# Down-projections of a two-layer encoder trunk: block sums T2 and T4 formed in the up-projections, last operands loaded earlier and split later

## Chip, cores and metric

The kernel runs on one core of a Trainium2 chip. The metric is the device time of one execution in microseconds (us), the median of several runs. The engines are PE (matrix multiplications, with PEld for the loading of its weights), DVE (VectorE, element by element on two operands), ACT (ScalarE, here mostly rounding copies), POOL (GpSimd, here almost only the issuer of accumulating transfers) and SP (the issuer of all other transfers). Each takes its own instructions in order and waits for the others by semaphores.

## What is computed

A sequence of 1024 frames of width 1024 goes through two layers. Each ends in a gated MLP with a causal convolution:

```python
def conv_ffn(h, w_up, conv_w, conv_b, w_down):
    s = h.shape[1]
    u = h @ w_up
    up = jnp.pad(u, ((0, 0), (CONV_WIDTH - 1, 0), (0, 0)))
    conv = conv_b
    for j in range(CONV_WIDTH):
        conv = conv + conv_w[j] * up[:, j:j + s]
    a, g = jnp.split(conv, 2, axis=-1)
    return (jax.nn.silu(a) * g) @ w_down

def reference(...):
    for layer in range(DEPTH):
        ...
        x = x + conv_ffn(rms_norm(x, ffn_norm[layer]), ffn_w_up[layer], ffn_conv_w[layer],
                         ffn_conv_b[layer], ffn_w_down[layer])
    return x
```

The hidden width is 2816, that is 22 blocks of 128 rows. The rest (a stick-breaking attention with a pooling mixer in layer 0, a gated linear attention in layer 1) is not touched here.

## The kernel before

**Splitting.** Every factor of a product is held as a rounded high part and a low part (float32 less the rounded value). A product is three matmuls: high by high, high by low, low by high. A *split* is one CAST on ACT (the high part) and one subtraction on DVE (the low part), in this order.

**Seven products instead of eight.** Both the up- and the down-projection treat their factors as 2x2 blocks and compute seven block products (Winograd's form). For the down-projection the blocks of the right factor are the halves in time (T0, T1, 512 frames each) of an even and an odd block of the hidden layer. With B11 and B12 the halves of the even block and B21 and B22 those of the odd one, the sums are T1 = B12 - B11, T3 = B22 - B12, T2 = T3 + B11 and T4 = T3 + (B11 - B21). A product sums over 11 pairs of blocks, j = 0 to 10.

**Up-projection, `ffn`.** The loop over i makes hidden block i by seven products on PE (class `Pair`, lines 979 to 1005 evacuate them), the convolution (L1038 on ACT, L1039 and L1041 on DVE) and the gate. In an even i, L1175 makes `even` and L1176 T1; B11 and T1 are written to DRAM. In an odd i, L1182 makes the odd block in `ca`, L1183 U = B11 - B21 and L1184 T3, both in `cg`; L1186 writes B21 and B22 as one tile `b2` and L1187 writes U and T3 as one tile `ut3`. One i lasts about 19.4 us.

**Down-projection, `down`.** `order` runs through six products P1, P5, P6, P3, P7, P4, each with steps j = 0 to 10: 66 steps of 12 matmuls (L1266). `prep` of step number i + 3 is written ahead of step i: it fetches the operands (L1211, tags `rb` for the right block, `rw`, `rs` and `ra` for the left ones, four buffers each for `rb` and `rw`), forms the left operand on DVE (`left`: L1226 for P5, L1229 for P6, L1235 for P3, L1237 for P7) and splits both in `split_block` (L1195 ACT, L1196 DVE) into tiles `blk` of a pool of 16 buffers. The right operand comes from the table `right`. Where the table names two sources, the second is added in flight: POOL issues an accumulating transfer (L1213) that has to wait until the first one has landed. P6 takes T3 and adds B11; P4 takes T3 and adds U.

The seventh product needs, as its left operand, four *rows* of the odd weight blocks (`last_left`, L1293 to L1295; a tile `wraw` of 8 blocks and a tile `r3` of 3, in pieces of 512 bytes) and as its right operand the eleven B21 (`last_right`, L1278 to L1282, two at a time). Rows 0 and 1 are loaded and split at P6's steps 2 and 6; the B21 from P7's step 8 to P4's step 7. The final loop multiplies them (L153 to L157).

When a product's 11 steps are done, four additions (eight behind P7) put its PSUM banks into x (L1270).

**Order.** PE follows the program as written throughout, and SP does so inside `down`. ACT and DVE are ordered by a scheduler that works from its own estimate of the times when the program is built. So a change in one place can move instructions on DVE and ACT elsewhere.

Of the kernel before, what the change touches and what calls it, by code (L numbers as in the profile page):

```python
# [57 lines left out]
def trunk_kernel(  # L58
# [952 lines left out]
    def ffn(layer, nm, after, ow, mixt, onward=None):  # L1011
# [107 lines left out]
        for i in range(FT):  # L1119
            nx = i + 1 < FT  # L1120
            ca, cg = cs_[2 * i % 3], cs_[(2 * i + 1) % 3]
            if i == 0:
                ua, ug = us[0], us[1]
            elif i == 1:
                ua, ug = us[2], us[0]
                for cs, b in zip(HALVES, ps):
                    V.tensor_tensor(ug[:, cs], b, rstd_bc[:, cs], op=ALU.mult)
            else:
                further = i + 2 < FT
                if i == 2:  # L1130
# [24 lines left out]
                scaled(ug[:, T0], T0)  # L1155
                q, p = p, None
                if nx:
                    p = Pair(i + 1)
                    p.P1()
                q.P3()  # L1160
                if nx:
                    split_s34()
                if further:
                    load_s4(i + 2)
                scaled(ua[:, T1], T1)
            if i == 1:
                for ld in loads:
                    ld(i + 2)
            conv(FT + i, ug, cg)
            conv(i, ua, ca)  # L1170
            S.activation(ca, ca, AF.Silu)


            if i % 2 == 0:
                V.tensor_tensor(even, ca, cg, op=ALU.mult)  # L1175
                V.tensor_tensor(ca[:, T0], even[:, T1], even[:, T0], op=ALU.subtract)  # L1176
                b11, t1 = (dram.tile([P, 512], F32, tag=f"{n}{layer}_{i}", name=n) for n in ("b11", "t1"))
                nc.sync.dma_start(b11, even[:, T0])
                nc.sync.dma_start(t1, ca[:, T0])
                blocks.append({"B11": b11, "T1": t1})  # L1180
            else:
                V.tensor_tensor(ca, ca, cg, op=ALU.mult)  # L1182
                V.tensor_tensor(cg[:, T0], even[:, T0], ca[:, T0], op=ALU.subtract)  # L1183
                V.tensor_tensor(cg[:, T1], ca[:, T1], even[:, T1], op=ALU.subtract)  # L1184
                b2, ut3 = (dram.tile([P, T], F32, tag=f"{n}{layer}_{i}", name=n) for n in ("b2", "ut3"))
                nc.sync.dma_start(b2, ca)  # L1186
                nc.sync.dma_start(ut3, cg)  # L1187
                blocks[-1].update(B21=b2[:, T0], B22=b2[:, T1], U=ut3[:, T0], T3=ut3[:, T1])
        ev.close()

        down(layer, blocks, ready, after, onward)

    def split_block(src):
        t = hpool.tile([P, T], R32, tag="h", name="blk")
        S.copy(t[:, 0:512], src)  # L1195
        V.tensor_sub(t[:, 512:T], src, t[:, 0:512].bitcast(F32))  # L1196
        return t

    def down(layer, blocks, ready, after, onward):

# [5 lines left out]
        NJ = FT // 2  # L1206
        w = [(wdn[layer, 2 * j], wdn[layer, 2 * j + 1]) for j in range(NJ)]

        def fetched(tag, src, add=None, bufs=4):
            t = dn.tile([P, 544 if tag == "rb" else 512], F32, tag=tag, name=tag, bufs=bufs)[:, 0:src.free_size()]  # L1210
            nc.sync.dma_start(t, src)  # L1211
            if add is not None:
                G.dma_start(t, add, accum_op=ALU.add)  # L1213
            return t

        a11, s = [None] * NJ, [None] * NJ
# [20 lines left out]
                V.tensor_tensor(t, a11[j], t, op=ALU.subtract)  # L1237
            return t


        right = {"P1": ("B11",), "P5": ("T1",), "P6": ("T3", "B11"), "P3": ("B22",), "P7": ("T3",), "P4": ("T3", "U")}

        def prep(n, j):
            if n == "P1" and j < len(ready):
                return ready[j]
            rb = fetched("rb", *(blocks[j][b] for b in right[n]))
            if n == "P1":
                load_a11(j)
            return split_block(left(n, j)), split_block(rb)
# [23 lines left out]
        b21 = []  # L1273

        def last_right(js):
            raw = hpool.tile([P, T], R32, tag="h", name="b21").bitcast(F32)
            for cs, j in zip(HALVES, js):
                nc.sync.dma_start(raw[:, cs], blocks[j]["B21"])  # L1278
                hi = dn.tile([P, 512], R32, tag="ra", name="b21h", bufs=NJ)
                lo = dn.tile([P, 512], R32, tag="rs", name="b21l", bufs=NJ)  # L1280
                S.copy(hi, raw[:, cs])
                V.tensor_sub(lo, raw[:, cs], hi.bitcast(F32))  # L1282
                b21.append((hi, lo))

        odd = wdn[layer].rearrange("(f two) p k -> two p f k", two=2)[1]

        def last_left(r):
            parts = []
            big = (hpool, ("wraw", "h", "h"), (1, 16, 16)) if r == KT // 2 - 1 else (wpool, ("wraw", "whi", "wlo"), (1, 2, 2))
            for k0, k1, (pool, tags, nb) in ((0, KT, big), (KT, NJ, (dn, ("r3", "r3h", "r3l"), (1, 2, 2)))):  # L1290
                raw, hi, lo = ((wpool if t == "wraw" else pool).tile([P, (k1 - k0) * P], d, tag=t, name=t, bufs=b)
                               for t, d, b in zip(tags, (F32, R32, R32), nb))
                nc.sync.dma_start(raw.rearrange("p (f k) -> p f k", k=P), odd[:, k0:k1, r * P:(r + 1) * P])  # L1293
                S.copy(hi, raw)
                V.tensor_sub(lo, raw, hi.bitcast(F32))  # L1295
                parts += [(hi[:, sl], lo[:, sl]) for sl in (slice(k * P, (k + 1) * P) for k in range(k1 - k0))]
            return parts
# [47 lines left out]
        for r in range(half):  # L1345
# [389 lines left out]
```

## Time and profile before

| | us |
|---|---|
| median of 3 runs | 2199.06 (2197.35 to 2202.14) |
| the profiled execution | 2199.35 |
| its span in the profile | 2197.7 |
| up-projection and down-projection, layer 0 | up from about 494, six products of `down` from 881.4 |
| up-projection and down-projection, layer 1 | up from about 1570, six products of `down` from 1968.5 |
| granted TensorE clock, mean | 0.996 |

All times below are microseconds from the span's start. A row of the timeline has start, duration, engine, line, operation, output and inputs, form, count; in brackets stands the idle time of the engine ahead of it and what ended it. Durations overlap: an instruction starts before the one ahead of it has fully ended, so the distance between starts, not the duration, is what a queue of them costs. A row of the waits has who waited for whom, the total in us, how often, and the longest.

### The profile page before, as it was taken

How to read it: one execution, taken by the hardware profiler on the slowest of the kernel's cores; microseconds unless marked ns; L12 is line 12 of the kernel's file. 1: busy time of each engine (PE TensorE's matmuls, PEld its weight loads, DVE VectorE, ACT ScalarE, POOL GpSimd, SP SyncE). 2: the span in 40 equal slices, each digit the busy share in tenths (PEclk: the TensorE clock that was granted, in tenths of full speed). 3: DMA queues.
4: the chain of work that ended last, by engine and by line, in shares of the span. 5: the costliest groups of instructions: out<-in, count | busy, mean ns of one | idle time of the engine just before them, and what ended most of it. 6: DMA issues, size and time to landing. Idle time of an engine off the chain costs nothing.

```text
span 2197.7 us, 28082 instructions
## 1 busy us (share of the span) xinstructions
PE 2150.8 (98%) x10384; PEld 1767.0 (80%) x10384; DVE 1664.8 (76%) x2458; ACT 1093.1 (50%) x1705; POOL 162.1 (7%) x188
## 2 busy tenths in 40 slices
PE   8999989999999999999999999999999999999998
PEld 7889878888878888778887878787788888887776
DVE  5687688698989899777736655557898998987763
ACT  6666566464444444344546362637544444443441
POOL 2240120000000000010000000000000000000110
PEclk9999999999999999999999999999999999999999
DMA  4132332353444434987501111105343444449885
GB/s 152 49 107 87 94 112 94 119 130 106 130 119 126 124 116 124 350 216 233 169 21 40 38 49 38 49 30 145 105 124 116 123 122 120 124 157 327 222 239 157
DMA packets 126201, 280.31 MB, mean 128 GB/s; under 512 B 13408, under 2 KB 27360, under 8 KB 126064
## 3 DMA queue, kind: packets, MB, share of 16 engines
q1 hardware_dynamic: 112528, 251.25, 34.9%
q0 software_dynamic: 13536, 27.27, 7.0%
q8 instruction: 81, 1.33, 0.2%
q14 instruction: 56, 0.46, 0.1%
HBM read 208.21 MB, written 54.53 MB: 120 GB/s over the span
## 4 chain that ended last, share of the span: by engine, by line
PE 61%; DMA 15%; DVE 15%; issue 4%; ACT 4%; SPq 1%; POOL 0%; DVEq 0%; ACTq 0%; POOLq 0%
PE lin L936 10%; PE z L936 7%; PE lin L153 4%; PE lin L155 4%; PE lin L157 4%; DMA rb<-ut 4%; PE t L936 3%; PE d L936 3%; DMA rw<-in_wdn 3%; DVE blk L1196 2%; PE z L157 2%; PE z L153 2%; PE z L155 2%; DMA raw_g<-in_wup 2%; DMA wraw<-in_wup 2%
## 5 line engine op out<-in xcount | busy, mean ns | idle before, releaser
L1038 ACT ACTIVATE c<-u,prm 128x1024 f32<-128x1024 f32 x88 | 109.1, 1244 | 86.7 <-DVE u L964 79.1
L1266 PE MATMUL lin<-blk 128*128 128x512 f32 x396 | 118.6, 400 | 14.0 <-ACT blk L1195 8.6
L1196 DVE TENSOR_TENSOR blk<-rb,blk 128x512 fp32r<-128x512 f32 x124 | 85.1, 686 | 53.9 <-ACT blk L1195 53.4
L153 PE MATMUL lin<-h_hi,whi 128*128 128x512 f32 x288 | 114.2, 432 | 6.6 <-ACT whi L139 6.0
L1039 DVE SCALAR_TENSOR_TENSOR c<-u,prm,c 128x1023 f32<-128x1023 f32 x88 | 112.3, 1278 | 8.5 <-ACT c L1038 8.5
L1195 ACT CAST blk<-rb 128x512 fp32r<-128x512 f32 x124 | 76.6, 618 | 81.2 <-DMA rb<-ut 44.0
L936 PE MATMUL d<-T,a 128*128 128x512 f32 x480 | 115.4, 389 | 0.0
L1041 DVE SCALAR_TENSOR_TENSOR c<-u,prm,c 128x1022 f32<-128x1022 f32 x88 | 112.3, 1276 | 0.0
L1266 PE MATMUL t<-blk 128*128 128x512 f32 x396 | 112.0, 391 | 0.0
L1266 PE MATMUL d<-blk 128*128 128x512 f32 x396 | 111.9, 391 | 0.0
L1266 PE MATMUL z<-blk 128*128 128x512 f32 x396 | 111.6, 390 | 0.0
L964 DVE TENSOR_TENSOR u<-u,rstd_bc 128x512 f32<-128x512 f32 x160 | 107.8, 684 | 0.4
L936 PEld LDWEIGHTS d<-T,a 128*128 128x128 f32 x480 | 90.1, 188 | 18.7
L155 PE MATMUL lin<-h_lo,whi 128*128 128x512 f32 x288 | 104.4, 398 | 0.7 <-DVE h_lo L264 0.7
L1266 PEld LDWEIGHTS lin<-blk 128*128 128x128 f32 x396 | 73.0, 189 | 39.8 <-ACT blk L1195 13.2
L157 PE MATMUL lin<-h_hi,wlo 128*128 128x512 f32 x288 | 104.2, 398 | 0.0
L936 PE MATMUL z<-blk,s34h 128*128 128x512 f32 x320 | 101.3, 398 | 1.4 <-DVE u L995 1.4
L936 PE MATMUL z<-blk,s12h 128*128 128x512 f32 x320 | 100.9, 396 | 0.0
L936 PE MATMUL lin<-T,s34h 128*128 128x512 f32 x320 | 99.5, 392 | 0.8 <-ACT tm L986 0.8
L936 PE MATMUL t<-blk,whi 128*128 128x512 f32 x320 | 99.6, 392 | 0.0
L936 PE MATMUL lin<-blk,whi 128*128 128x512 f32 x320 | 99.5, 392 | 0.0
L936 PE MATMUL lin<-T,s12h 128*128 128x512 f32 x320 | 99.4, 391 | 0.0
(516 smaller groups left out, 6021.0 us busy)
## 6 DMA issues: line engine op xcount, KB each, us to landing
wraw<-in_wup SPq DMA_DIRECT2D x44, 512.0 KB, 3.7
rw<-in_wdn SPq DMA_DIRECT2D x88, 256.0 KB, 4.7
raw_g<-in_wup SPq DMA_DIRECT2D x40, 512.0 KB, 3.8
rb<-ut SPq DMA_DIRECT2D x66, 256.0 KB, 4.4
b<-c SPq DMA_DIRECT2D x22, 512.0 KB, 2.6
ut<-c SPq DMA_DIRECT2D x22, 512.0 KB, 3.8
s<-in_wup SPq DMA_DIRECT2D x40, 256.0 KB, 2.6
s<-s POOLq DMA_DIRECT2D x40, 256.0 KB, 4.4
```

The source lines that it names most:

```text
L153: PE.matmul(out[i], wh, ah[i], start=first, stop=False)
L155: PE.matmul(out[i], wh, al[i], start=False, stop=False)
L157: PE.matmul(out[i], wl, ah[i], start=False, stop=last)
L936: PE.matmul(ps, w, m, start=first and k == 0 and n == 0, stop=k == 3 and n == 2, skip_group_check=True)
L964: V.tensor_tensor(dst, dst, rstd_bc[:, cs], op=ALU.mult)
L1038: S.activation(c, u, AF.Identity, scale=pcol(b + 2), bias=pcol(b + 3))
L1039: V.scalar_tensor_tensor(c[:, 1:], u[:, :T - 1], pcol(b + 1), c[:, 1:], op0=ALU.mult, op1=ALU.add)
L1041: V.scalar_tensor_tensor(c[:, 2:], u[:, :T - 2], pcol(b), c[:, 2:], op0=ALU.mult, op1=ALU.add)
L1195: S.copy(t[:, 0:512], src)
L1196: V.tensor_sub(t[:, 512:T], src, t[:, 0:512].bitcast(F32))
L1266: PE.matmul(ps, l, m, start=first and j == 0 and i == 0, stop=j == NJ - 1 and i == 2, skip_group_check=True)
```

## The change

Three parts. First, the odd i of the up-projection forms T4 = U + T3 in place of U and T2 = B11 + T3 in place of `even`'s first half, by two more additions on DVE, and writes T4 and T3 as one tile `t43` and T2 as a tile `t2` of its own. The table `right` then has one source per product, and the accumulating transfers of `down` are gone. Second, `last_left` and `last_right` only issue their transfers and return a function `later` that does the splits. Row 0 is loaded at P5's step 6 and split at P6's step 6, row 1 loaded at P3's step 1 and split at P3's step 10 (rows 2 and 3, in the final loop, are split at once as before). The B21 are loaded from P7's step 2 on and split four steps later, from P7's step 6 to P4's step 5. Third, these splits are traced inside `behind_latest`, which puts them on ACT and DVE behind the split of the latest `prep`. That is an order of issue alone; nothing waits for the completion of the split ahead.

```diff
+                V.tensor_tensor(cg[:, T0], cg[:, T0], cg[:, T1], op=ALU.add)
+                V.tensor_tensor(even[:, T0], even[:, T0], cg[:, T1], op=ALU.add)
-                nc.sync.dma_start(ut3, cg)
-                blocks[-1].update(B21=b2[:, T0], B22=b2[:, T1], U=ut3[:, T0], T3=ut3[:, T1])
+                nc.sync.dma_start(t43, cg)
+                nc.sync.dma_start(t2, even[:, T0])
+                blocks[-1].update(B21=b2[:, T0], B22=b2[:, T1], T4=t43[:, T0], T3=t43[:, T1], T2=t2)
...
     def split_block(src):
-        S.copy(t[:, 0:512], src)
-        V.tensor_sub(t[:, 512:T], src, t[:, 0:512].bitcast(F32))
+        a = S.copy(t[:, 0:512], src)
+        b = V.tensor_sub(t[:, 512:T], src, t[:, 0:512].bitcast(F32))
+        latest[:] = a.ins, b.ins
...
+    def behind_latest():
+        st = ExitStack()
+        for ins in latest:
+            st.enter_context(tc.issue_after(ins))
+        return st
...
-            if add is not None:
-                G.dma_start(t, add, accum_op=ALU.add)
...
-        right = {"P1": ("B11",), "P5": ("T1",), "P6": ("T3", "B11"), "P3": ("B22",), "P7": ("T3",), "P4": ("T3", "U")}
+        right = {"P1": "B11", "P5": "T1", "P6": "T2", "P3": "B22", "P7": "T3", "P4": "T4"}
...
-            if n == "P6" and j in (2, 6):
-                rows[j // 4] = last_left(j // 4)
-            k = NJ * (n == "P4") + j - 8
-            if n in ("P7", "P4") and k % 2 == 0 and 0 <= k < NJ + 1:
-                last_right(range(k, min(k + 2, NJ)))
+            if (n, j) in LATER:
+                with behind_latest():
+                    due.pop(0)()
+            if (n, j) in ROWS:
+                due.append(last_left(ROWS.index((n, j))))
+            k = NJ * (n == "P4") + j - 2
+            if n in ("P7", "P4") and k % 2 == 0 and 0 <= k < NJ + 5:
+                if k > 3:
+                    with behind_latest():
+                        due.pop(0)()
+                if k < NJ + 1:
+                    due.append(last_right(range(k, min(k + 2, NJ))))
```

with `ROWS, LATER = [("P5", 6), ("P3", 1)], [("P6", 6), ("P3", 10)]`. Lines of the changed kernel are shifted: L1195, L1196 of `split_block` become L1199, L1200; L1211 becomes L1225; L1226 and L1229 become L1238 and L1241; L1270 becomes L1281; L1293 to L1295 become L1309 to L1318.

Three places where the order of instructions moves. SP, from the last steps of P5 in layer 0 into P6, before (`t` are the T1, `ut` the tiles with T3):

```order
L1211 DMA rb<-t_7423 128x512
L1211 DMA rs<-in_wdn 128x512
L1211 DMA rw<-in_wdn 128x512
L1211 DMA rb<-ut_4931 128x512
L1211 DMA rb<-ut_5209 128x512
L1211 DMA rb<-ut_5470 128x512
L1211 DMA rb<-ut_5731 128x512
L1211 DMA rb<-ut_5992 128x512
L1211 DMA rb<-ut_6253 128x512
L1293 DMA wraw<-in_wdn 128x8x128
L1293 DMA r_8168<-in_wdn 128x3x128
```

and now (`t_4934` and on are the T2):

```order
L1225 DMA rw<-in_wdn 128x512
L1309 DMA wraw<-in_wdn 128x8x128
L1309 DMA r_8047<-in_wdn 128x3x128
L1225 DMA rb<-t_7463 128x512
L1225 DMA rs<-in_wdn 128x512
L1225 DMA rw<-in_wdn 128x512
L1225 DMA rb<-t_4934 128x512
L1225 DMA rb<-t_5216 128x512
L1225 DMA rb<-t_5481 128x512
```

Row 0's two transfers now stand ahead of the three of P5's last step (j = 10) and of all of P6's.

ACT in P6 of layer 0 (`blk<-rs` and `blk<-rb` are a step's two splits), before:

```order
L1195 CAST blk<-rs 128x512
L1294 CAST whi<-wraw 128x1024
L1195 CAST blk<-rb 128x512
L1195 CAST blk<-rs 128x512
L1294 CAST r3h<-r_8168 128x384
L1195 CAST blk<-rb 128x512
L1195 CAST blk<-rs 128x512
```

and now:

```order
L1199 CAST blk<-rb 128x512
L1317 CAST whi<-wraw 128x1024
L1317 CAST r3h<-r_8047 128x384
L1199 CAST blk<-rs 128x512
L1199 CAST blk<-rb 128x512
L1199 CAST blk<-rw 128x512
```

Before, row 0 was split between the casts of P6's steps 4 and 5; now between those of its steps 9 and 10, the last ahead of P3's first (`blk<-rw`).

DVE at the start of P5 in layer 0 (`rs<-rs,rw` forms a step's left operand for P5, `rs<-rs,ra` the one for P6 later, `x<-x,...` are the four additions behind P1), before:

```order
L1229 TENSOR_TENSOR rs<-rs,ra 128x512
L1270 TENSOR_TENSOR x<-x,lin 128x512
L1226 TENSOR_TENSOR rs<-rs,rw 128x512
L1270 TENSOR_TENSOR x<-x,z 128x512
L1270 TENSOR_TENSOR x<-x,t 128x512
L1270 TENSOR_TENSOR x<-x,d 128x512
L1196 TENSOR_TENSOR blk<-rs,blk 128x512
L1196 TENSOR_TENSOR blk<-rb,blk 128x512
L1226 TENSOR_TENSOR rs<-rs,rw 128x512
L1229 TENSOR_TENSOR rs<-rs,ra 128x512
L1196 TENSOR_TENSOR blk<-rs,blk 128x512
L1226 TENSOR_TENSOR rs<-rs,rw 128x512
```

and now:

```order
L1238 TENSOR_TENSOR rs<-rs,rw 128x512
L1200 TENSOR_TENSOR blk<-rs,blk 128x512
L1200 TENSOR_TENSOR blk<-rb,blk 128x512
L1241 TENSOR_TENSOR rs<-rs,ra 128x512
L1281 TENSOR_TENSOR x<-x,lin 128x512
L1281 TENSOR_TENSOR x<-x,z 128x512
L1281 TENSOR_TENSOR x<-x,t 128x512
L1281 TENSOR_TENSOR x<-x,d 128x512
L1238 TENSOR_TENSOR rs<-rs,rw 128x512
L1200 TENSOR_TENSOR blk<-rs,blk 128x512
L1200 TENSOR_TENSOR blk<-rb,blk 128x512
L1238 TENSOR_TENSOR rs<-rs,rw 128x512
```

Step 1 is now split ahead of the additions, and step 2's left operand is formed only behind all four.

More of the change, by code (lines that the diff above doesn't have):

```diff
@@ L1184, in ffn @@
                 V.tensor_tensor(cg[:, T1], ca[:, T1], even[:, T1], op=ALU.subtract)
-                b2, ut3 = (dram.tile([P, T], F32, tag=f"{n}{layer}_{i}", name=n) for n in ("b2", "ut3"))
+                V.tensor_tensor(cg[:, T0], cg[:, T0], cg[:, T1], op=ALU.add)
+                V.tensor_tensor(even[:, T0], even[:, T0], cg[:, T1], op=ALU.add)
+                b2, t43, t2 = (dram.tile([P, n], F32, tag=f"{s}{layer}_{i}", name=s)
+                               for s, n in (("b2", T), ("t43", T), ("t2", 512)))
                 nc.sync.dma_start(b2, ca)
-                nc.sync.dma_start(ut3, cg)
-                blocks[-1].update(B21=b2[:, T0], B22=b2[:, T1], U=ut3[:, T0], T3=ut3[:, T1])
+                nc.sync.dma_start(t43, cg)
+                nc.sync.dma_start(t2, even[:, T0])
+                blocks[-1].update(B21=b2[:, T0], B22=b2[:, T1], T4=t43[:, T0], T3=t43[:, T1], T2=t2)
         ev.close()
@@ L1245, in prep @@
                 return ready[j]
-            rb = fetched("rb", *(blocks[j][b] for b in right[n]))
+            rb = fetched("rb", blocks[j][right[n]])
             if n == "P1":
@@ L1278, in last_right, with later @@
                 nc.sync.dma_start(raw[:, cs], blocks[j]["B21"])
[L1279 to L1283, printed above, removed]
+            def later():
+                for cs, j in zip(HALVES, js):
+                    hi = dn.tile([P, 512], R32, tag="ra", name="b21h", bufs=NJ)
+                    lo = dn.tile([P, 512], R32, tag="rs", name="b21l", bufs=NJ)
+                    S.copy(hi, raw[:, cs])
+                    V.tensor_sub(lo, raw[:, cs], hi.bitcast(F32))
+                    b21.append((hi, lo))
@@ L1285, in down @@
+            return later
         odd = wdn[layer].rearrange("(f two) p k -> two p f k", two=2)[1]
         def last_left(r):
-            parts = []
             big = (hpool, ("wraw", "h", "h"), (1, 16, 16)) if r == KT // 2 - 1 else (wpool, ("wraw", "whi", "wlo"), (1, 2, 2))
+            raws = []
             for k0, k1, (pool, tags, nb) in ((0, KT, big), (KT, NJ, (dn, ("r3", "r3h", "r3l"), (1, 2, 2)))):
-                raw, hi, lo = ((wpool if t == "wraw" else pool).tile([P, (k1 - k0) * P], d, tag=t, name=t, bufs=b)
-                               for t, d, b in zip(tags, (F32, R32, R32), nb))
+                raw = (wpool if tags[0] == "wraw" else pool).tile([P, (k1 - k0) * P], F32, tag=tags[0], name=tags[0], bufs=1)
@@ L1293, in last_left, with later @@
                 nc.sync.dma_start(raw.rearrange("p (f k) -> p f k", k=P), odd[:, k0:k1, r * P:(r + 1) * P])
[L1294 to L1297, printed above, removed]
+                raws.append((raw, pool, tags, nb))
+            def later():
+                parts = []
+                for raw, pool, tags, nb in raws:
+                    n = raw.free_size()
+                    hi, lo = (pool.tile([P, n], R32, tag=t, name=t, bufs=b) for t, b in zip(tags[1:], nb[1:]))
+                    S.copy(hi, raw)
+                    V.tensor_sub(lo, raw, hi.bitcast(F32))
+                    parts += [(hi[:, sl], lo[:, sl]) for sl in (slice(k * P, (k + 1) * P) for k in range(n // P))]
+                rows[r] = parts
@@ L1299, in down @@
+            return later
         LEAD = 3
@@ L1305, in down @@
         half = KT // 2
-        rows = {}
+        rows, due = {}, []
+        ROWS, LATER = [("P5", 6), ("P3", 1)], [("P6", 6), ("P3", 10)]
         for i, (n, j) in enumerate(order):
@@ L1350, in down @@
             if r + 2 < half:
-                rows[r + 2] = last_left(r + 2)
+                last_left(r + 2)()
             if r == 0:
```

3 lines of the change are left out of this document (2 added, 1 removed).

## The prediction

> **What bounds the kernel now.** I read the page first, then PE's timeline at the ends of the products, then who waits.
>
> ```profile
> span 2197.7 us, 28082 instructions
> PE 2150.8 (98%) x10384; PEld 1767.0 (80%) x10384; DVE 1664.8 (76%) x2458; ACT 1093.1 (50%) x1705; POOL 162.1 (7%) x188
> ```
>
> PE is busy for 98% of the span, so a change that leaves the matmuls alone can only win what PE loses in gaps. Its timeline gives these gaps by product: the first matmul of P5, P6, P3, P7, P4 and of the final loop (L153) in layer 0, then P5, P6, P3, P4 and the final loop in layer 1.
>
> ```profile
> 911.30 0.84 PE L1266 MATMUL lin<-blk 128*128 128x512 f32 x3
> 943.80 0.84 PE L1266 MATMUL lin<-blk 128*128 128x512 f32 x3
> 980.81 0.84 PE L1266 MATMUL lin<-blk 128*128 128x512 f32 x3
> 1010.73 0.84 PE L1266 MATMUL lin<-blk 128*128 128x512 f32 x3
> 1040.65 0.84 PE L1266 MATMUL lin<-blk 128*128 128x512 f32 x3
> 1071.27 0.40 PE L153 MATMUL lin<-b21h,whi 128*128 128x512 f32 x1
> ...
> 1998.47 0.84 PE L1266 MATMUL lin<-blk 128*128 128x512 f32 x3
> 2030.41 0.84 PE L1266 MATMUL lin<-blk 128*128 128x512 f32 x3
> 2066.53 0.84 PE L1266 MATMUL lin<-blk 128*128 128x512 f32 x3
> 2126.37 0.84 PE L1266 MATMUL lin<-blk 128*128 128x512 f32 x3
> 2162.43 0.40 PE L153 MATMUL lin<-b21h,whi 128*128 128x512 f32 x1
> ```
>
> P3 and P7 in layer 0 take 980.81 to 1010.73 and 1010.73 to 1040.65, both 29.92 for 11 steps, 2.72 a step: PE without a gap. What the others take above 29.92 is lost. Layer 0: P5 32.50, so **2.6**; P6 37.01, **7.1**; P4 30.62, **0.7**. Layer 1: P5 31.94, **2.0**; P6 36.12, **6.2**; P4 36.06, **6.1**. Together 24.7 us. That is all there is to win in these products, and the three parts of the change aim at P6 and P4.
>
> **Why P6 and P4 lose.** Two of the waits inside layer 1's six products:
>
> ```profile
> POOL rb L1213 <- DMA rb<-ut: 29.6, 10, 4.5
> ACT blk L1195 <- DMA rb<-ut: 25.0, 11, 7.4
> ```
>
> POOL waits 29.6 us for the first source of a right operand before it may issue the second (up to 4.5 each); ACT then waits 25.0 for the accumulating transfer (in P4 it too is named `rb<-ut`), up to 7.4. A right block is thus two landings, up to 11.9 of waiting, and has one of four `rb` buffers meanwhile: 11.9 / 4 is over PE's 2.72. That is P4's bound and the base of P6's. P6 has a second burden; ACT, PE and a window of layer 0:
>
> ```profile
> 966.54 1.05 ACT L1294 CAST whi<-wraw 128x1024 fp32r<-128x1024 f32 x1 [1.38 <-DMA wraw<-in_wdn]
> 969.72 0.62 ACT L1195 CAST blk<-rb 128x512 fp32r<-128x512 f32 x1 [2.13 <-DMA rb<-b]
> 970.39 0.50 PE L1266 MATMUL lin<-blk 128*128 128x512 f32 x1 [2.08 <-ACT blk L1195]
> 972.00:1002.00 30.00, 30.00 (x127) 24.66 (x126) 26.81 (x45) 15.90 (x29) 0.00 (x0) 0.94 0.74 234
> ```
>
> Row 1's split sits at the head of ACT's queue and waits 1.38 for its row, with a step's casts behind it; PE stands for 2.08 at 970.39. Behind that gap the granted clock is 0.94 over 30 us (last row, third number from the end): 0.06 x 30 = 1.8 of the 7.1 are slow matmuls.
>
> The Trainium skill's "TensorE: Matmul & The Clock Gate", Part 1, says that the clock is gated down after an idle window of about 3.4 us. This trace shows it behind a gap of 2.08. By the page those 1.8 would have another cause and could stay: the sum below would come out 1.8 higher.
>
> **Part by part.**
>
> *Accumulating transfers gone (22 per layer).*
>
> ```profile
> rb<-ut SPq DMA_DIRECT2D x66, 256.0 KB, 4.4
> ```
>
> A right block is one landing again, 4.4 by the page's median, as in P3 and P7, which have the same splits, one more DVE operation per step, and lose nothing. P6 then fetches one block of 256 KB a step where P3 fetches two. POOL has no other work in `down`. I take P4's loss (0.7 + 6.1) as gone, and P6's with the next item. Ends: none of it, or all, 20.1 with P6.
>
> *Rows 0 and 1 split behind later steps.* Same instructions, so no new work; their rows have long landed, so ACT no longer waits with casts behind it. P6's 7.1 + 6.2 = 13.3 goes. What is late next: at P6's start the splits have little lead, but without transfers to wait for a split pair is 1.2 on DVE against 2.72 on PE, so the lead grows each step. Behind the moved splits on ACT and DVE stand P6's step 10 and P3's step 0, some steps ahead of PE by then.
>
> *Row 0's load moved into P5.* It stands on SP ahead of the loads of P5's step 10 and all of P6's. A row's landing in layer 1's tail (last number), the DMA engines at P5's end in layer 0 (share 0.28), and step 10's left operand, from issue to landing and then on DVE:
>
> ```profile
> wraw<-in_wdn SPq DMA_DIRECT2D x1, 512.0 KB, 5.2
> 934.00:936.00 2.00, 1.77 (x8) 1.18 (x7) 2.00 (x4) 1.08 (x3) 0.00 (x0) 1.00 0.28 106
> 930.03 3.89 DMA rw<-in_wdn
> 936.79 0.68 DVE L1226 TENSOR_TENSOR rs<-rs,rw 128x512 f32<-128x512 f32 x1
> ```
>
> Step 10's `rw` landed at 933.92 and DVE took it at 936.79, 2.9 spare. If the row holds step 10 up for its full landing of 5.2, it costs 5.2 - 2.9 = 2.3 a layer; at the other end nothing. I take nothing: DVE itself is later there (next item), and part of the row fits into that idle stretch. Row 1 and the B21 move into P3 and P7, whose steps need 2.72 on PE with the DMA share at 0.74 (the 972 to 1002 row): nothing, up to 2.3 a layer if not.
>
> *DVE's order in P5.* P5's loss is not the transfers': DVE waits for one only twice, at its first steps. That wait, then DVE from step 6 to 7 and at step 8, then PE at step 8, all in layer 0:
>
> ```profile
> DVE rs L1226 <- DMA rw<-in_wdn: 3.1, 2, 2.7
> 926.41 0.69 DVE L1226 TENSOR_TENSOR rs<-rs,rw 128x512 f32<-128x512 f32 x1
> 927.86 0.69 DVE L1196 TENSOR_TENSOR blk<-rs,blk 128x512 fp32r<-128x512 f32 x1 [0.76 <-ACT blk L1195]
> 928.47 0.69 DVE L1196 TENSOR_TENSOR blk<-rb,blk 128x512 fp32r<-128x512 f32 x1
> 929.07 0.69 DVE L1229 TENSOR_TENSOR rs<-rs,ra 128x512 f32<-128x512 f32 x1
> 929.67 0.68 DVE L1226 TENSOR_TENSOR rs<-rs,rw 128x512 f32<-128x512 f32 x1
> ...
> 934.99 0.68 DVE L1196 TENSOR_TENSOR blk<-rb,blk 128x512 fp32r<-128x512 f32 x1
> 935.73 0.73 PE L1266 MATMUL lin<-blk 128*128 128x512 f32 x2 [0.23 <-DVE blk L1196]
> ```
>
> A sum followed at once by its own split waits 1.45 (926.41 to 927.86) for ACT's cast in between, and the step costs 929.67 - 926.41 = 3.26 against PE's 2.72: 0.54 lost. With another operation in between it costs 0.60 per operation. PE's second matmul starts 0.74 behind the start of the right block's subtraction (934.99 to 935.73). Before, steps 4 to 7 were of the slow kind. The new order has 1, 2, 4 to 7 and 10, and all four additions to x ahead of step 2's sum. Laid out from the same first landing with these distances, layer 0's right blocks of steps 2, 4 and 8 are subtracted at 917.1, 923.0 and 936.0, and the last of P5 lets P6 start at 944.7, 0.9 later than 943.80. The same for layer 1 gives 2030.8 against 2030.41, **+0.4**. So +1.3. Ends: all eleven steps slow, 11 x 0.54 = 5.9 a layer, +3.3 and +3.9; or P5 without loss, -4.6. I take the layout, as the order is fixed when the program is built.
>
> *The two additions.* 22 pairs x 2 x 0.60 = 22 x 1.2 = 26.4 us of DVE in the up-projections. DVE in one odd i, and the window of one pair of i:
>
> ```profile
> 707.11 0.69 DVE L1184 TENSOR_TENSOR c<-c,even 128x512 f32<-128x512 f32 x1
> 707.71 0.69 DVE L964 TENSOR_TENSOR u<-u,rstd_bc 128x512 f32<-128x512 f32 x1
> 709.73 0.69 DVE L1005 TENSOR_TENSOR u<-tm,z 128x512 f32<-128x512 f32 x1 [1.33 <-PE z L936]
> 708.00:747.00 39.00, 39.00 (x171) 31.68 (x170) 35.19 (x44) 17.63 (x20) 1.72 (x2) 1.00 0.41 122
> ```
>
> Distance between two such operations is 0.60 (707.11 to 707.71). In the new order they stand just ahead of L1005, where DVE waits 1.33 for PE: 1.2 fits, and DVE has 3.8 of 39 free per pair. Cost 0; the cover is that wait, and without it 26.4 less the free time, which the rival below prices. On SP the writes of T4, T3 and T2 stand ahead of the next loads of `s` and `wraw`, whose buffers are freed later on DVE anyway. SP issues one transfer more per pair. The last pair's T2 stands among P5's first loads; a step of P5 fetches three blocks of its size in at most 3.26, so it holds them up by an estimate of 1.1 at most, within the 2.9 spare above.
>
> **Sum**, against the profiled execution of 2199.35 (span 2197.7 and 1.65 around it; 0.3 above the median of 2199.06): -13.3 - 6.8 + 1.3 = -18.8. I leave 0.5 a layer for single waits such as P4's 0.7 in layer 0: -17.8, so 2181.5.
>
> **Rivals.** *P5 and the row (0.15):* the row's load and T2 hold up P5's end by 2.3 a layer, and the steps of P5 run slow to the upper end, half of 7.2: gain 17.8 - 4.6 - 2.3 to 3.6, about 11, time **2188**. For it: P5 fetches three blocks a step, the most of the six; against it: the 2.9 spare.
> *P4 keeps its loss (0.08):* its waits come not from the second landing but from DVE, which has eight additions behind P7 and now B21 splits among the splits: gain 17.8 - 6.8 = 11, **2188**. Against it: P4 in layer 0 has the same additions and lost 0.7.
> *The change does not do what it says (0.06):* P6 waits for `rb` as such, four buffers and SP's queue, and only the clock loss and a little more goes: gain 2 to 4, **2196**.
> *The other side (0.06):* DVE becomes the bound of the up-projections. Per pair of i it has 3.8 free. It takes 1.2 more, and the new order puts `s34l`, which waits for ACT's cast, right behind L1005. It decides once what these waits add passes 3.8 - 1.2 = 2.6 a pair. If the additions are then paid in full, 26.4 - 18.8 = +7.6, **2207**. Against it: the 1.33 in the row, at the place where the additions go.
>
> **How the numbers follow.** Forecast 0.65, 2181.5, its own range 2176 to 2187 from the ends (-24.7 all gone, P5 +3 more). With the first two rivals 2176 to 2192 holds about 0.83. 0.2% is 4.4 us, what a measurement of this kernel can tell from no change: faster 0.88, within 0.07, slower 0.05.
>
> **What would show it.** Right: the starts of P6 to P3 and of P4 to the final loop 29.9 to 30.5 apart in both layers; POOL without L1213; ACT's row casts with no idle time before them; no clock under 1.00 in the six products; P5 32 to 34. Wrong: PE waiting at L936 for DVE in the up-projections, SP's or ACT's waits for `rb` in P6, P5 over 36.

## The result and the profile after

| | before | after |
|---|---|---|
| median, us | 2198.20 (4 runs) | 2178.06 (2176.42 to 2179.50, 4 runs) |
| ratio, 95% interval | 1 | 0.9907 (0.9890 to 0.9924) |
| profiled execution, us | 2199.35 | 2178.09 |
| span, us | 2197.7 | 2176.4 |

The changed kernel is 20.1 us faster; forecast were 17.6 (2181.5 against 2199.06, the median of the three runs known then). Two runs among all that follow were in a slow state (2756.20 of the kernel before, 6272.64 of `p5_ahead_again`), and no median here contains them. The top of the page of the changed kernel:

```profile
span 2176.4 us, 28046 instructions
PE 2141.7 (98%) x10384; PEld 1766.4 (81%) x10384; DVE 1689.8 (78%) x2502; ACT 1093.3 (50%) x1705; POOL 123.7 (6%) x144
```

DVE has 44 more instructions, the two additions in 22 odd i, and is busy for 25 us more; POOL has 44 fewer, the accumulating transfers. PE's timeline of the changed kernel at the starts of P1, P5, P6, P3, P7, P4 and the final loop in layer 0, then of P6, P3, P7, P4 and the final loop in layer 1:

```profile
880.04 0.86 PE L1277 MATMUL lin<-blk 128*128 128x512 f32 x3
909.98 0.84 PE L1277 MATMUL lin<-blk 128*128 128x512 f32 x3
942.42 0.84 PE L1277 MATMUL lin<-blk 128*128 128x512 f32 x3
972.34 0.84 PE L1277 MATMUL lin<-blk 128*128 128x512 f32 x3
1002.26 0.84 PE L1277 MATMUL lin<-blk 128*128 128x512 f32 x3
1032.18 0.84 PE L1277 MATMUL lin<-blk 128*128 128x512 f32 x3
1062.10 0.40 PE L153 MATMUL lin<-b21h,whi 128*128 128x512 f32 x1
...
2021.35 0.84 PE L1277 MATMUL lin<-blk 128*128 128x512 f32 x3
2051.27 0.84 PE L1277 MATMUL lin<-blk 128*128 128x512 f32 x3
2081.19 0.84 PE L1277 MATMUL lin<-blk 128*128 128x512 f32 x3
2111.11 0.84 PE L1277 MATMUL lin<-blk 128*128 128x512 f32 x3
2141.03 0.40 PE L153 MATMUL lin<-b21h,whi 128*128 128x512 f32 x1
```

From P6's start on, every distance is 29.92: PE has no gap at all in P6, P3, P7 and P4 of either layer. Only P5 still loses, 32.44 less 29.92 = 2.5 in layer 0. The sequence from P1 to the final loop takes 182.06 in layer 0 (189.91 before) and 181.34 in layer 1 (193.93): 7.85 + 12.59 = 20.4 of the 21.3 us between the two profiled executions. The other 0.8 lies outside the six products: layer 0's P1 starts 1.3 earlier (880.04 for 881.36), and 0.5 of that is lost again later. In ten of the eleven other profiled executions below layer 0's P1 starts anywhere from 877.6 to 884.4, so such a distance says nothing of the change.

ACT's wait for right blocks in layer 1's six products of the changed kernel:

```profile
ACT blk L1199 <- DMA rb<-t: 4.0, 5, 2.3
```

Then ACT's timeline in layer 0's P6, the two casts of row 0:

```profile
953.21 1.05 ACT L1317 CAST whi<-wraw 128x1024 fp32r<-128x1024 f32 x1
954.16 0.51 ACT L1317 CAST r3h<-r 128x384 fp32r<-128x384 f32 x1
```

And the window of that P6:

```profile
942.00:972.00 30.00, 30.00 (x134) 24.86 (x133) 25.88 (x42) 16.85 (x30) 0.00 (x0) 1.00 0.74 231
```

The waits for right blocks are 4.0 with 2.3 the longest, where before they were 25.0 and 7.4 in the same place. No bracket stands behind the row's casts, so ACT did not wait for the row. The granted clock is 1.00 (third number from the end of the window's row). All this is as forecast, but for two of the prediction's signs. P5 was to take 32 to 34 and takes 31.7 in layer 1 (1989.63 to 2021.35). And ACT's waits for `rb` in P6, named as a sign of being wrong, are there: the 4.0 all lie in layer 1's P6, and layer 0's P6 has 3.7. PE has no gap behind them, so the sign was badly chosen. What the profile does not tell is which of the three parts did it.

### The profile page after: what moved, and what is told of

It is laid out like the page before. It is cut to its first block, busy times and chain, and to the rows that moved or that the text cites. A ratio compares the mean times of both kernels' runs of the same rounds, so it can differ in the third digit from the quotient of the medians.

```text
span 2176.4 us, 28046 instructions
## 1 busy us (share of the span) xinstructions
PE 2141.7 (98%) x10384; PEld 1766.4 (81%) x10384; DVE 1689.8 (78%) x2502; ACT 1093.3 (50%) x1705; POOL 123.7 (6%) x144
## 4 chain that ended last, share of the span: by engine, by line
PE 82%; DVE 6%; DMA 6%; ACT 4%; issue 2%; SPq 0%; POOL 0%; ACTq 0%; DVEq 0%; POOLq 0%
PE lin L936 15%; PE z L936 10%; PE d L936 5%; PE t L936 5%; PE lin L153 4%; PE lin L155 4%; PE lin L157 4%; PE lin L1277 3%; PE z L1277 3%; PE d L1277 3%; PE t L1277 3%; PE z L157 2%; PE z L153 2%; PE z L155 2%; DMA x<-xs 1%
## 5 line engine op out<-in xcount | busy, mean ns | idle before, releaser
L936 PE MATMUL d<-T,a 128*128 128x512 f32 x480 | 115.4, 389 | 0.0
L1277 PE MATMUL lin<-blk 128*128 128x512 f32 x396 | 113.6, 392 | 1.6 <-DVE blk L1200 1.6
L936 PEld LDWEIGHTS d<-T,a 128*128 128x128 f32 x480 | 90.1, 188 | 18.7
L936 PE MATMUL z<-blk,s34h 128*128 128x512 f32 x320 | 101.1, 397 | 1.2 <-DVE u L995 1.2
L936 PE MATMUL lin<-T,s34h 128*128 128x512 f32 x320 | 99.6, 392 | 1.5 <-ACT tm L986 1.5
L936 PE MATMUL z<-blk,s12h 128*128 128x512 f32 x320 | 100.9, 396 | 0.0
L936 PE MATMUL t<-blk,whi 128*128 128x512 f32 x320 | 99.6, 392 | 0.0
L936 PE MATMUL lin<-blk,whi 128*128 128x512 f32 x320 | 99.5, 392 | 0.0
L936 PE MATMUL lin<-T,s12h 128*128 128x512 f32 x320 | 99.3, 391 | 0.0
L139 ACT CAST whi<-wraw 128x1024 fp32r<-128x1024 f32 (+2 forms) x57 | 57.1, 1003 | 80.7 <-PE z L155 21.7
L1199 ACT CAST blk<-rw 128x512 fp32r<-128x512 f32 x66 | 41.0, 621 | 95.2 <-DVE rw L1249 43.4
```

Of the source, the lines that this page charges most:

```text
L139: S.copy(hi[:, cs], raw[:, cs])
L936: PE.matmul(ps, w, m, start=first and k == 0 and n == 0, stop=k == 3 and n == 2, skip_group_check=True)
L1199: a = S.copy(t[:, 0:512], src)
L1277: PE.matmul(ps, l, m, start=first and j == 0 and i == 0, stop=j == NJ - 1 and i == 2, skip_group_check=True)
```

## The experiments

For each kernel, what its profiled execution loses beyond 29.92 in a product (P1, P3 and P7 lose nothing in any), layer 0 / layer 1, and its time. A time is compared with the kernel before on the same chip, and in the last three rows also with one another. The kernel before took 2199.65 beside `sums_only`, `late_only`, `adds2` and `p5_ahead`, 2198.78 beside `no_queue`, `adds4`, `x_plus1` and `sums_ahead`, and 2198.88 beside the last three:

| kernel | P5 | P6 | P4 | median, us | ratio to before, 95% interval |
|---|---|---|---|---|---|
| before | 2.6 / 2.0 | 7.1 / 6.2 | 0.7 / 6.1 | 2198.20 | 1 |
| changed | 2.5 / 1.8 | 0 / 0 | 0 / 0 | 2178.06 | 0.9907 (0.9890 to 0.9924) |
| sums_only | 3.4 / 1.4 | 0 / 0 | 0 / 0 | 2177.69 | 0.9899 (0.9876 to 0.9922) |
| late_only | 2.4 / 2.1 | 3.8 / 4.5 | 4.1 / 6.2 | 2194.48 | 0.9975 (0.9963 to 0.9986) |
| no_queue | 4.0 / 2.9 | 0 / 0 | 0 / 0 | 2179.54 | 0.9911 (0.9894 to 0.9927) |
| adds2 | 3.7 / 4.0 | 0 / 0 | 0 / 0 | 2180.95 | 0.9913 (0.9893 to 0.9932) |
| adds4 | 2.6 / 2.6 | 0 / 0 | 0 / 0 | 2195.03 | 0.9982 (0.9969 to 0.9995) |
| x_plus1 | 2.0 / 2.4 | 0 / 0 | 0 / 0 | 2176.67 | 0.9901 (0.9881 to 0.9921) |
| p5_ahead | 0.7 / 0.0 | 0 / 0 | 0 / 0 | 2172.87 | 0.9880 (0.9857 to 0.9904) |
| sums_ahead | 1.9 / 0.0 | 0 / 0 | 0 / 0 | 2175.61 | 0.9892 (0.9876 to 0.9909) |
| after_again | 3.7 / 1.5 | 0 / 0 | 0 / 0 | 2177.76 | 0.9902 (0.9882 to 0.9921) |
| sums_only_again | 2.7 / 1.8 | 0 / 0 | 0 / 0 | 2177.71 | 0.9902 (0.9882 to 0.9923) |
| p5_ahead_again | 2.2 / 0.0 | 0 / 0 | 0 / 0 | 2172.64 | 0.9886 (0.9865 to 0.9906) |

### The sums alone

To the kernel before, only the first part is added: the two additions, the tiles `t43` and `t2`, and

```diff
-        right = {"P1": ("B11",), "P5": ("T1",), "P6": ("T3", "B11"), ... "P4": ("T3", "U")}
+        right = {"P1": ("B11",), "P5": ("T1",), "P6": ("T2",), ... "P4": ("T4",)}
```

> The kernel before with the two additions in the up-projections and one source per product, so no accumulating transfers; rows and B21 are loaded and split where they were. Theory (as in the prediction): P4's loss of 0.7 + 6.1 goes, and the base of P6's; what is left of P6 is the row split that waits for its row at the head of ACT's queue, 1 to 3 us a layer in one or two gaps of PE. P6's lead is larger than before, so the gap may stay under the 2.08 behind which the clock was lower. Time before less 16 to 19. Rival (the rows alone make P6 slow): P6 keeps 5 us or more a layer and only P4's 6.8 goes: before less 7 to 9. Rival (it was the B21 splits that slowed P4): P4 of layer 1 keeps 3 us or more.

It gained the whole of it: P6 and P4 without a gap, 22.0 us below before. That is more than its theory, which left 1 to 3 us a layer in P6, and both rivals fall. ACT's timeline in P6 of layer 0 of this kernel, at its two row splits:

```profile
947.88 1.05 ACT L1298 CAST whi<-wraw 128x1024 fp32r<-128x1024 f32 x1 [0.58 <-DMA wraw<-in_wdn]
...
956.13 1.05 ACT L1298 CAST whi<-wraw 128x1024 fp32r<-128x1024 f32 x1 [2.38 <-DMA wraw<-in_wdn]
957.09 0.51 ACT L1298 CAST r3h<-r 128x384 fp32r<-128x384 f32 x1
957.50 0.61 ACT L1199 CAST blk<-rb 128x512 fp32r<-128x512 f32 x1
```

PE's start of P3 there:

```profile
973.40 0.84 PE L1270 MATMUL lin<-blk 128*128 128x512 f32 x3
```

The rows still make ACT wait at the head of its queue, 0.58 and 2.38, the second longer than the 1.38 shown before. But the block cast behind the second wait, at 957.50, is the one of P6's step 10, which PE takes 2.72 us ahead of P3, at 970.7: the lead, by which a cast is ahead of PE, is 13.2 us, and a wait of 2.4 is lost in it. Before, the cast behind the wait stood at 969.72 and PE took it at 970.39. So it was the lead that was missing, and with the accumulating transfers gone it is there.

The rows of the prediction say the same when the second bracket is read too. The cast at 969.72 waited 2.13 for its own accumulating transfer, after the row's cast was over, and PE's 2.08 ended with that cast. The DMA view of the kernel before has this transfer issued at 961.50 and landed 8.2 later, where the median of P6's eleven is 5.2. The row's two transfers were on the way in the same time (issued at 959.42 and 959.89, landed 7.1 and 7.8 later); that they slowed it is not shown. The row's split, then, did not end this wait of PE's. The chain of work that ended last does run through both rows' transfers there (945.89 to 954.38 and 959.42 to 966.52), so what the rows cost may lie in their loads. Two things are not separated by any run: a sum formed earlier takes away the second landing and also half the bytes of a right block (the share of the DMA engines in layer 0's P6 falls from 0.93 to 0.76, in its P4 from 0.94 to 0.55).

### The loads and the late splits alone

In the changed kernel the accumulating transfers are put back, as in the kernel before:

```diff
+            if add is not None:
+                G.dma_start(t, add, accum_op=ALU.add)
...
-        right = {"P1": "B11", "P5": "T1", "P6": "T2", "P3": "B22", "P7": "T3", "P4": "T4"}
+        right = {"P1": ("B11",), "P5": ("T1",), "P6": ("T3", "B11"), ... "P4": ("T3", "U")}
```

> The changed kernel with the accumulating transfers put back (U and T3 written as before, no T2 and T4, no additions); rows and B21 are loaded early and split late, as in the change. Theory (two landings bound a step at 11.9 / 4 = 2.98 against 2.72): P6 keeps about 3 us a layer without the clock loss, P4 keeps 0.7 and 6.1: before less 6 to 8. Rival (the rows alone): P6 is whole, before less 13. Rival (the B21 splits slow P4): P4 of layer 1 loses 3 us or more less than its 6.1.

It is 5.2 us below before, a little less than the theory's 6 to 8. P6 keeps 3.8 and 4.5, where the theory had about 3; the rival that had it whole falls, and so does the one that had layer 1's P4 lose 3 less. What the moved rows save there, loads and splits together, is 3.3 and 1.7, the clock's 1.8 among the first. But P4 got worse in layer 0, 4.1 for 0.7, which neither side expected. Waits of this kernel's P6 in layer 0:

```profile
POOL rb L1223 <- DMA rb<-ut: 20.1, 8, 5.7
ACT blk L1195 <- DMA rb<-b: 16.7, 10, 3.5
```

DVE's timeline from P4's first additions to step 3:

```profile
1036.95 1.28 DVE L1279 TENSOR_TENSOR x<-x,lin 128x512 f32<-128x512 f32 x2
...
1041.74 1.27 DVE L1279 TENSOR_TENSOR x<-x,d 128x512 f32<-128x512 f32 x2
1042.94 0.68 DVE L1196 TENSOR_TENSOR blk<-rw,blk 128x512 fp32r<-128x512 f32 x1
1043.54 0.68 DVE L1196 TENSOR_TENSOR blk<-rb,blk 128x512 fp32r<-128x512 f32 x1
```

PE's there and in layer 1's P4, with the gap in brackets:

```profile
1044.27 0.75 PE L1275 MATMUL lin<-blk 128*128 128x512 f32 x2 [2.23 <-DVE blk L1196]
2131.58 1.22 PE L1275 MATMUL lin<-blk 128*128 128x512 f32 x2 [3.38 <-DVE blk L1196]
```

And windows of two microseconds around the first (the fourth time in a row is DVE's busy time):

```profile
1042.00:1044.00 2.00, 0.04 (x1) 0.00 (x0) 2.00 (x4) 0.24 (x1) 0.00 (x0) 1.00 0.71 136
1044.00:1046.00 2.00, 1.73 (x5) 1.45 (x6) 2.00 (x5) 2.00 (x5) 0.86 (x1) 0.72 0.46 59
1046.00:1048.00 2.00, 2.00 (x6) 1.52 (x6) 2.00 (x5) 0.98 (x2) 0.00 (x0) 0.50 0.84 184
1048.00:1050.00 2.00, 2.00 (x10) 1.62 (x9) 0.43 (x1) 0.21 (x1) 0.86 (x1) 0.93 1.04 338
```

P6 waits for both landings as before. In P4 the eight additions behind P7, with two B21 subtractions among them and no split of a block, keep DVE fully busy from 1036.95 to 1042.94 while PE's next block waits for its subtraction: the wait that the prediction's rival for P4 (0.08) described. The cast of that block, step 3's right one, was done at 1039.24, after 0.75 of waiting for its second landing; PE's second matmul of the step, which takes the subtraction's result, was due at 1041.9. In the changed kernel splits stand between the additions, and the same subtraction starts at 1033.86, 6.5 ahead of PE. So two things differ, the lead, shorter with two landings, and the scheduler's order on DVE; which of them would have been enough is not shown. The gap of 2.23 then costs a second time: the clock is 0.50 at 1046 to 1048 and 4.1 are lost in all.

Layer 1's 6.2 agrees with the 6.1 before, and with the theory, in size alone. Here it is one gap of 3.38 behind the same additions and the slow clock after it (0.50 from 2132 to 2136, 0.72 in the next 2 us), which makes up the other 2.8. In the kernel before P4 of layer 1 has gaps of at most 0.81, the larger ones behind ACT's casts, and a clock of 1.00 throughout.

### More additions

Behind the two new additions of an odd i, two (adds2) or four (adds4) more, into the half of `even` that nothing reads any more:

```diff
+                for _ in range(2):
+                    V.tensor_tensor(even[:, T1], even[:, T0], cg[:, T1], op=ALU.add)
```

> The changed kernel with two more additions behind the two new ones in each odd i of the up-projections; they write the second half of the even block, which nothing reads any more. 22 x 2 x 0.60 = 26.4 us more of DVE. Theory (the cover is the time in which DVE stands idle in a pair, 39.0 less 36.6 = 2.4): cost 0 to 4 us against the changed kernel. Rival (the cover is only the wait ahead of L1005, of which 0.25 us of 1.33 is left): what is past it is paid, 22 x (1.2 - 0.25) = 21 us more than the changed kernel, with PE waiting at L936 for DVE.

> The changed kernel with four more additions in each odd i (2.4 us more of DVE a pair, 22 x 2.4 = 53 in all, written to the dead half of the even block). DVE is then busy for 36.6 + 2.4 = 39.0 of the 39.0 us of a pair. Theory (free time in a pair is the cover, and the point from which the additions are paid is 2.4): the up-projections grow by no more than 0.2 us a pair, 5 us in all; P5's start gets worse, as with two more. Rival (waits for ACT and PE in between cannot be filled, so a part of the 2.4 is paid): 0.5 us a pair or more, 11 us or more in the up-projections, with PE waiting at L936 for DVE.

The window from 560 to 850, about seven pairs of i, before, changed, with two more and with four more (the fourth time in a row is DVE's busy time):

```profile
560.00:850.00 290.00, 289.12 (x1253) 234.64 (x1252) 262.11 (x321) 130.24 (x149) 12.93 (x15) 1.00 0.41 121
```

```profile
560.00:850.00 290.00, 290.00 (x1258) 235.64 (x1257) 271.44 (x336) 132.19 (x150) 13.14 (x16) 1.00 0.43 129
```

```profile
560.00:850.00 290.00, 290.00 (x1256) 235.04 (x1255) 279.60 (x350) 131.09 (x150) 12.89 (x15) 1.00 0.43 129
```

```profile
560.00:850.00 290.00, 287.10 (x1235) 230.58 (x1234) 285.08 (x363) 126.37 (x147) 12.46 (x15) 1.00 0.43 127
```

PE's waits for DVE in layer 0's up-projection with four more:

```profile
PEld z L936 <- DVE u L995: 5.7, 8, 0.9
PE z L936 <- DVE u L995: 2.7, 6, 0.5
```

From the first matmul of L936 to P1's start, the up-projection took 389.31 and 390.28 before, 389.42 and 390.38 changed, 389.76 and 390.36 with two more, 397.36 and 396.34 with four more. So the change pays 0.1 a layer for its 26.4 us, and the same again costs next to nothing, as the theory of `adds2` had it. Its median is 2.9 above the changed kernel's; in its profile P5 loses 3.4 more, where the first sum starts 24.8 and 25.0 behind P1. With four more, 14 of the 53 us are paid, and the rival of `adds4` is right. A good part of it is one gap of PE in the last i of each layer, 2.16 at 883.12 and 2.45 at 1970.19 (0.18 and 1.04 in the changed kernel), and 1.7 of slow clock behind the first. The theory's limit, 2.4 a pair, was therefore too high: DVE had 4.9 of 290 idle and PE already stood still for it.

### Without the queueing

```diff
-                with behind_latest():
-                    due.pop(0)()
+                due.pop(0)()
```

at both places.

> The changed kernel without the queueing: the late splits of rows 0 and 1 and of the B21 are where the scheduler puts them; loads as in the change. Order on ACT: row 0's split stands some eleven steps' casts further ahead than in the change. Theory (since the sums alone made P6 and P4 whole, with 3 us of waits for rows at ACT's head and PE still without a gap, the queueing moves work that has room anyway): P6, P3, P7, P4 without loss, time within 3 us of the changed kernel. Rival (without the queueing a row split stands ahead of casts that PE needs soon, as in the kernel before): P6 loses 1 to 3 us a layer and the gain falls by 2 to 6.

The theory held for P6, P3, P7 and P4. But P5 loses 4.0 and 2.9, though its first sums start at 23.79 and 22.78 behind P1, much as in the changed kernel. DVE's timeline in layer 0 of this kernel shows row 0's split at P5's step 9, which PE starts at 937.53:

```profile
937.17 1.22 DVE L1318 TENSOR_TENSOR wlo<-wraw,whi 128x1024 fp32r<-128x1024 f32 x1
938.31 0.55 DVE L1318 TENSOR_TENSOR r3l<-r,r3h 128x384 fp32r<-128x384 f32 x1
```

PE loses 0.5 and 0.7 in steps 9 and 10, where the changed kernel loses nothing more. The median is 1.5 above the changed kernel's, no more than these runs can tell apart. What the queueing keeps away is thus a burden that loading row 0 in P5 has made possible; `sums_only`, which loads it in P6, has no such burden.

### When P5's first operand lands

The four loads of x in P1 stand one step later:

```diff
-            if n == "P1" and 2 <= j < 10:
-                load_a11(j - 2) if j < 6 else load_x(j - 6)
+            if n == "P1" and 2 <= j < 6:
+                load_a11(j - 2)
+            if n == "P1" and j >= 7:
+                load_x(j - 7)
```

> The changed kernel with the four loads of x in P1 one step later each, so that one of them less (512 KB) stands on SP ahead of P5's first operands. In the six products measured so far with the new order of DVE, P5's loss is the start of its first sum, counted from P1's start, less 21.0 to 21.1 (23.62 gave 2.52, 22.83 gave 1.80, 25.04 gave 4.01). Theory (P5's loss is set by when its first operand lands, and from there by DVE's order): the first sum starts 0.5 to 1.5 us earlier in layer 0, and P5's loss falls by the same amount, by 0.5 to 1.5. Rival (P5 is bound by later transfers, share of the DMA engines 0.92): the first sum moves and the loss stays at 2.5.

In layer 0 the first sum starts 22.43 behind P1 (23.62 in the changed kernel) and P5 loses 1.95, which is 0.6 less, not 1.2. In layer 1 it starts at 22.93 and P5 loses 2.41. Both follow one rule again, the start less 20.5: here DVE's order has another slow step (0.54), and that is the difference between 20.5 and 21.1. The landing does carry through, and the order is a second term beside it. That the moved load brought the landing forward is not shown: in layer 1 it came no earlier (22.83 in the changed kernel), and layer 0's differs by as much between executions of the changed kernel alone (23.62 and 24.83, below).

### P5's sums one step ahead

```diff
+            if n == "P5":
+                if j not in sums:
+                    left(n, j)
+                if j + 1 < NJ:
+                    left(n, j + 1)
+                with tc.issue_after(sums[min(j + 1, NJ - 1)]):
+                    wt = split_block(s[j])
+                return wt, split_block(rb)
```

> The changed kernel, but in P5 the sum for the left operand of step j + 1 is formed ahead of the split of step j, so that no sum stands directly ahead of its own split on DVE. Theory (what P5 still loses, 2.5 and 1.7 us, is DVE's 3.26 us a step where the sum waits 0.76 for ACT's cast): a step costs DVE four operations of 0.60 = 2.4, P5 takes 29.9 to 30.6, and the kernel is 3 to 4.2 us below the changed one. Rival (P5 is bound by its three transfers a step, DMA share 0.9): the idle time moves from ACT's casts to the sums, which wait for rw, and P5 stays at 31.5 or more; 0 to 1 us gained.

Its median is 5.2 us below the changed kernel's, with P5 at 30.6 and 29.9. The theory's size holds and is even passed, its mechanism holds only in part. DVE's timeline in the middle of P5 in layer 1 of this kernel:

```profile
2001.71 0.69 DVE L1238 TENSOR_TENSOR rs<-rs,rw 128x512 f32<-128x512 f32 x1
2002.32 0.68 DVE L1200 TENSOR_TENSOR blk<-rs,blk 128x512 fp32r<-128x512 f32 x1
2003.04 0.69 DVE L1241 TENSOR_TENSOR rs<-rs,ra 128x512 f32<-128x512 f32 x1
2004.27 0.69 DVE L1200 TENSOR_TENSOR blk<-rb,blk 128x512 fp32r<-128x512 f32 x1 [0.54 <-ACT blk L1199]
2005.04 0.69 DVE L1238 TENSOR_TENSOR rs<-rs,rw 128x512 f32<-128x512 f32 x1
```

ACT's cast of the right block there:

```profile
2003.62 0.62 ACT L1199 CAST blk<-rb 128x512 fp32r<-128x512 f32 x1 [0.48 <-DMA rb<-t]
```

And the window of that whole P5 (the last number but one is the share of the DMA engines):

```profile
1981.00:2021.00 40.00, 40.00 (x178) 33.10 (x177) 34.56 (x55) 17.94 (x31) 0.00 (x0) 1.00 0.97 349
```

The wait of 0.76 behind a sum is gone, but such a step still takes 2005.04 - 2001.71 = 3.33, since now the right block lands late (0.48, then 0.54 on DVE) and the DMA engines are busy for 0.97. Where the time was won is the start, in this P5 and the changed kernel's: the sum of step 2 no longer stands behind the four additions to x, and the right block of step 2 is subtracted 31.7 behind P1's start instead of 33.8. Its left split does still stand behind them, at 33.1, but PE multiplies by the left block's low part only in its third matmul, and by the right one's in its second. So step 2 is ready 0.8 earlier as a whole and 2.1 earlier in its right block, and P5 lives on that lead to its end. The transfers, three a step, are then the next thing that is waited for in the middle of P5, though at the right block and not, as the rival had it, at the sums.

> The kernel before with the sums T2 and T4 (as sums_only) and with P5's sum of step j + 1 ahead of the split of step j (as p5_ahead), so without the moved loads and splits. Theory (the gain of the change is the sums alone, and P5's loss is DVE's order): six products of a layer lose under 1 us, time within 3 us of p5_ahead, 24 to 28 below the kernel before. Rival (the moved splits are needed once P5 no longer gives P6 its lead, since P5 now ends 2 us earlier against the transfers): P6 loses 1 us or more a layer, 20 to 23 below before.

P6 stayed whole, which settles against the rival. The median is 2.7 above that of `p5_ahead`, on another chip, and 23.2 below before, a little less than the theory's 24 to 28; layer 0's P5 loses 1.9, where the theory had under 1. In this order too P5's loss follows the landing: it is 0.7, 1.9 and 2.2 in the three executions whose first sum in layer 0 starts at 23.25, 24.98 and 25.20 (`p5_ahead`, `sums_ahead`, `p5_ahead_again`), and nothing in layer 1, where it starts at 22.2 to 22.7.

### Side by side

> The changed kernel once more, beside the two that follow, on one chip. 0.990 to 0.992 of the kernel before.

> The kernel before with the sums alone, once more. Theory (the moved loads and splits are worth nothing once the accumulating transfers are gone): within 2 us of the changed kernel beside it. Rival (they are worth the 2 us that single runs on other chips hide): 2 to 4 us above the changed kernel.

> The changed kernel with P5's sums one step ahead, once more. Theory (P5's loss of 2.5 and 1.8 us goes, 0.7 stays): 3 to 4.5 us below the changed kernel beside it. Rival (the first measurement, 5.2 below, was of another chip): within 2 us of the changed kernel.

On one chip: 2177.76, 2177.71 and 2172.64. The sums alone are worth as much as the whole change, to within the 2 us or so that six runs can tell. `p5_ahead` has the lowest median, 5.1 us below the changed kernel, over the theory's 3 to 4.5. How much it gains is less sure: the ranges overlap (2172.57 to 2177.05 against 2174.24 to 2180.30), and its two profiled executions, 2177.29 and 2177.05, are the slowest of their groups.

## Why the prediction was right, point by point

**Accumulating transfers.** Right, at the upper end that the step named: "none of it, or all, 20.1 with P6". The sums alone took 6.8 from P4 and 13.3 from P6. That a step is bound at 11.9 / 4 is not shown: P4 of `late_only` has both landings and no gap but the one behind DVE's additions, and landing and bytes went together.

**Rows 0 and 1.** This is the step that failed as an explanation, though its sum came out. It said of the moved splits "P6's 7.1 + 6.2 = 13.3 goes". Moved alone they took 3.3 + 1.7 from P6 and gave 3.5 back in P4; with the sums there they add nothing (2177.76 against 2177.71). The prediction read the row's wait at 966.54 as a second burden of P6 with a price of its own. Without the accumulating transfers a longer wait of the same kind, 2.38, cost nothing, and even before the gap at 970.39 ended with a landing and not with the row's split. The sum of 13.3 was right because the first part was worth all of it.

**The clock.** Right: with no gap in P6 the clock is 1.00 there, so the 1.8 went.

**Row 0's load in P5.** Right at nothing, though the spare was misread: 3.89 is a piece of the chain that leads to the sum of step 9 at 934.38. From issue to landing the DMA view has 5.0 for this `rw`, so it landed at 935.0 and 1.8 were spare, not 2.9; the upper end would have been 3.4. It was not needed: P5's loss follows the same rule (below) whether the row is loaded in P5 or, in sums_only, in P6. The rival that put P5 and the row at 2188 falls.

**DVE's order in P5.** The slow steps were where the order showed them, and forecast was +0.9 and +0.4; the profile shows -0.1 and -0.2. The mis-sized term is the landing that the layout started "from the same first landing". Start of the first sum, counted from P1's start, beside P5's loss, in kernels with this order:

```
changed          23.62  2.52   22.83  1.80
sums_only        24.49  3.36   22.42  1.37
adds2            24.77  3.71   25.04  3.99
after_again      24.83  3.67   22.57  1.47
sums_only_again  23.79  2.65   22.91  1.79
```

(layer 0 left, layer 1 right.) Loss is start less 21.0 to 21.2 in all ten. For the kernel before it is 24.75 less 22.2 and 23.71 less 21.7. At the same landing the new order costs 1.1 and 0.7, a little over the forecast; the first operand landed 1.1 and 0.9 earlier and gave it back. In layer 0 the same program has 23.62 in one execution and 24.83 in another, so there it is scatter, and luck for the sum. In layer 1 it is more than that: the four executions here without the extra additions are at 22.4 to 22.9, and so are the other kernels with the sums and without extra additions (22.2 to 22.9), while the two kernels with accumulating transfers have 23.71 and 24.19. Why was not tried.

**The two additions.** Right at nothing (0.1 a layer). The other side's rival was no rival for this change, but its point was too far out: the prediction had 2.6 a pair beyond the change, and the runs put it between 1.2 (free) and 2.4, where 14 of 53 us are paid and not, as the rival had it, all.

**The sum.** 17.8 was forecast, against the profiled execution, and 20.4 found in the six products: 1.6 are P5's term, 1.0 the reserve of 0.5 a layer for single waits, of which none was left. The rival that the change does not do what it says, and the one that P4 keeps its loss, fall with P4 and P6 at 29.92.

## What to carry to other kernels

Two waits in one product are not two prices: ask which of them uses up the lead, since with that one gone the other may cost nothing, as the row splits here, whose waits went on and were no longer seen. A part of a change that is sound by itself should be run alone before it is credited. And a layout of an in-order queue is good to a few tenths of a microsecond, but only from a landing that is itself uncertain by one.

## What the runs showed of the hardware

The granted clock went to half behind single gaps of PE of 1.6 to 3.4 us. A gap of 2.23 at 1044.27 gave 0.50 in the window from 1046 to 1048 above; the 2.08 before the change gave 0.57 in the two windows from 972 to 976 of the kernel before:

```profile
970.00:972.00 2.00, 1.39 (x5) 0.92 (x6) 1.63 (x3) 1.56 (x4) 0.00 (x0) 1.00 1.02 247
972.00:974.00 2.00, 2.00 (x7) 1.56 (x6) 1.77 (x4) 0.99 (x3) 0.00 (x0) 0.57 0.90 261
974.00:976.00 2.00, 2.00 (x6) 1.59 (x6) 1.75 (x4) 1.57 (x4) 0.00 (x0) 0.57 0.87 267
976.00:978.00 2.00, 2.00 (x10) 1.64 (x10) 2.00 (x4) 1.08 (x2) 0.00 (x0) 1.00 0.78 229
```

The length of the gap alone does not decide. In the kernel before a gap of 1.57, far ahead of the products, is followed by 0.50:

```profile
241.10 0.39 PE L756 MATMUL d<-atl,vt 128*128 128x256 f32 x1 [1.57 <-DVE atl L744]
242.00:244.00 2.00, 2.00 (x6) 1.52 (x6) 1.28 (x5) 1.36 (x3) 0.00 (x0) 0.50 0.91 354
```

while its gap of 1.82 in layer 1, at 2057.76, left the clock at 1.00, and so did one of 2.45 in `adds4`:

```profile
1970.19 0.73 PE L936 MATMUL z<-blk,s34h 128*128 128x512 f32 x2 [2.45 <-DVE u L995]
```

What decides instead was not tried. Behind gaps of 1.57 to 2.23 the slow stretch costs 1.7 (2 x 2 x 0.43 in the windows above), about as much as the gap itself; that is 3.4 us at half speed. Behind the 3.38 of `late_only` it cost 2.8. The Trainium skill's "TensorE: Matmul & The Clock Gate", Part 1, has half speed and a window of about 3.4 us until full speed; both agree with these rows. That it also asks for an idle window of about 3.4 us does not: 1.57 was enough here.
